# Batched transposed matmul on one core: loading the first batch of a ahead of the first pair of b, and opening the critical section through GpSimd

## Chip, cores, metric

One NeuronCore of one Trainium2 chip. The metric is the device time of one execution in microseconds (us), as the median of several runs; it is about 1.8 us longer than the span that the profiler records (124.78 us and 123.0 us for the same execution of the kernel before). Ratios are the mean time of one kernel's fast runs over that of the other's fast runs of the same rounds, so not quite the ratio of the medians that are quoted beside them.

## The reference

```python
batch, m, k, n = 16, 512, 512, 512
a: (batch, k, m) float32;  b: (batch, n, k) float32
return np.matmul(a.transpose(0, 2, 1), b.transpose(0, 2, 1)).astype(np.float32)
```

It reads 16.8 MB of a and 16.8 MB of b and writes 16.8 MB: 50.33 MB.

## The kernel before

Sixteen batches. b comes in pairs of batches (2.1 MB, rows of 16 KB), a in single batches (1.05 MB, rows of 8 KB). VectorE casts b to bf16, TensorE transposes it, VectorE copies the transpose back; ScalarE casts a; TensorE multiplies; ScalarE and VectorE copy the products out, and a pair of outputs is stored at once. There are buffers for 4 batches of a, 3 pairs of b and 5 pairs of outputs. Everything is in one critical section, a part of the program that one engine opens and closes for all of them, and in which the engines wait for each other by hand-written semaphores (counters). A transfer is asked for by an "issue" on SyncE's or ScalarE's queue, and has "landed" when its semaphore says so. The parts that matter here (cuts are marked):

```python
    with tc.tile_critical():                       # the section; opened and closed by SyncE by default
        ...
        def run_sp(sp):                            # SyncE issues all loads and the last stores
            for i in range(B):
                for p in ([0] if i == 0 else [(i + 1) // 2] if i % 2 and i + 1 < B else []):
                    if p >= PAIRS:
                        sp.wait_ge(turned, p - PAIRS + 1)
                    sp.dma_start(b_sb[p % PAIRS][:], b_v[p]).then_inc(b_in[p % PAIRS], 16)
                s, use = i % LOADS, i // LOADS
                if use:
                    sp.wait_ge(summed, MO * (i - LOADS) + 1)
                if i % 2 == 0 and i // 2 >= OUTS:
                    sp.wait_ge(o_out[i // 2 % OUTS], 16 * (i // 2 // OUTS))
                sp.dma_start(a_sb[s][:], a_v[i]).then_inc(a_in[s], 16)
            ...                                    # stores 5, 6, and 7 in two halves
            sp.reg_mov(all_stored, 16 * STORED)
        ...
        def run_act(act):
            cast_a(act, 0)
            for i in range(B - 1):
                cast_a(act, i + 1)
                copy_out(act, i, slice(2, 4), oa_go)
                j, odd = divmod(i - LAG, 2)        # LAG = 3
                if odd and 0 <= j < H - TAIL:
                    store(act, j)                  # stores 0 to 4, on ScalarE's queue
            ...
    nc.sync.wait_ge(stored, nc.sync.snap(all_stored))   # behind the section: the last stores
```

## Time and profile before

| | before |
|---|---|
| median, range of 6 runs | 124.97 us, 124.70 to 125.09 |
| PE / VectorE / ScalarE busy | 70% / 46% / 38% |
| moved, mean rate over the span | 50.33 MB, 409 GB/s |
| rate from 4 us to 120 us, in 2 us bins | 417 to 432 GB/s, one stretch at 403 |
| first issue, first packet, last packet, last landing, end | 0.949, 1.956, 121.450, 121.934, 122.985 us |

No compute engine is full and the DMA engines are, from the second of 40 equal slices of the span to the last but one. The table's last row is the useful one: the span is a start, 50.33 MB at the full rate, and an end.

### The profile page before, as it was taken

Reading aid. Unit: us, or ns where it says so; the run is one execution under the profiler, and the core shown is the slowest. Engines: PE = TensorE matmul, PEld = TensorE weight load, DVE = VectorE, ACT = ScalarE, POOL = GpSimd, SP = SyncE. Lnnn points to the kernel's source line nnn. Section 1 sums busy time; section 2 is a strip of 40 time slices with the busy share of each in tenths; the row PEclk is TensorE's granted clock in tenths of the full one; section 3 lists DMA queues with packets and bytes.
Section 4 is the critical chain, followed back from the end, with each engine's and each line's share of the span. In section 5 each row is a group of like instructions: output and inputs, shape, how many; then the busy total and the mean of one; then the engine's idle time right before and its main releaser. Section 6 shows DMA issues by size and latency. Waiting matters only on the chain. (4 is left out here: it accounts for less than half of the span.)

```text
span 123.0 us, 1086 instructions
## 1 busy us (share of the span) xinstructions
PE 86.1 (70%) x400; PEld 49.7 (40%) x400; DVE 56.4 (46%) x48; ACT 46.8 (38%) x34; POOL 0.7 (1%) x6
## 2 busy tenths in 40 slices
PE   0006497997999799779930799965992679979600
PEld 0006344642755464346410546442640526437300
DVE  0016368478295755917039107780719306171200
ACT  4003209537717903176300950329230490750300
POOL 2000000000000000000000000000000000000000
PEclk9999999999999999999995557999999558999995
DMA  4999999999999999999999999999999999999992
GB/s 91 394 400 458 400 424 456 429 394 456 426 397 448 434 376 432 426 440 440 416 421 429 458 408 418 429 426 437 453 397 432 426 426 426 429 426 426 429 424 115
DMA packets 5648, 50.33 MB, mean 409 GB/s; under 512 B 528, under 2 KB 528, under 8 KB 528
## 3 DMA queue, kind: packets, MB, share of 16 engines
q1 hardware_dynamic: 4288, 39.85, 77.2%
q10 hardware_dynamic: 1360, 10.49, 20.1%
HBM read 33.55 MB, written 16.78 MB: 409 GB/s over the span
## 5 line engine op out<-in xcount | busy, mean ns | idle before, releaser
L219 PE MATMUL o_ps<-bt_sb,a_bf 128*128 128x512 bf16 x256 | 65.1, 403 | 7.1 <-PEq L194 6.6
L135 ACT CAST a_bf<-a_sb 128x2048 bf16<-128x2048 f32 x16 | 30.4, 1900 | 40.8 <-DMA a_sb<-in_a_dram 40.8
L219 PEld LDWEIGHTS o_ps<-bt_sb,a_bf 128*128 128x128 bf16 x256 | 28.5, 115 | 37.5 <-issue 15.0
L205 PE MATMUL bt_ps<-identity,b_bf 128*128 128x128 f32 x144 | 24.3, 323 | 22.7 <-PEq L194 22.7
L144 DVE COPY o_sb<-o_ps 128x1024 f32<-128x1024 f32 x16 | 19.6, 1224 | 35.8 <-PE o_ps L219 35.8
L205 PEld LDWEIGHTS bt_ps<-identity,b_bf 128*128 128x128 f32 x144 | 22.2, 212 | 28.2 <-issue 27.2
L152 DVE CAST b_bf<-b_sb 128x2048 bf16<-128x2048 f32 x16 | 19.5, 1221 | 19.1 <-DMA b_sb<-in_b_dram 19.1
L144 ACT COPY o_sb<-o_ps 128x1024 f32<-128x1024 f32 (+1 forms) x17 | 16.4, 962 | 28.0 <-PE o_ps L219 28.0
L161 DVE COPY bt_sb<-bt_ps 128x1024 f32<-128x1024 f32 x16 | 19.5, 1216 | 3.1 <-PE bt_ps L205 3.1
L135 ACT ACT_TABLE_LOAD x1 | 1.3, 1283 | 0.9 <-SPq L51 0.9
L122 POOL TENSOR_SCALAR_AFFINE_SELECT identity<-identity 128x128 f32<-128x128 f32 x1 | 0.3, 294 | 0.2 <-POOL identity L120 0.2
L120 POOL MEMSET identity<- 128x128 f32 x1 | 0.2, 205 | 0.7 <-SPq L51 0.7
L265 POOL MEMSET const-bfloat16-1.0<- 128x1 bf16 x1 | 0.1, 102 | 0.0
L265 POOL MEMSET const-uint8-127<- 128x1 uint8 x1 | 0.1, 102 | 0.0
L265 POOL MEMSET const-float32-0.0<- 128x1 f32 x1 | 0.1, 99 | 0.2 <-issue 0.2
L265 POOL MEMSET const-float32-1.0<- 128x1 f32 x1 | 0.1, 99 | 0.0
## 6 DMA issues: line engine op xcount, KB each, us to landing
b_sb<-in_b_dram SPq DMA_DIRECT2D x8, 2048.0 KB, 20.4
a_sb<-in_a_dram SPq DMA_DIRECT2D x16, 1024.0 KB, 17.5
out_dram<-o_sb ACTq DMA_DIRECT2D x5, 2048.0 KB, 15.2
out_dram<-o_sb SPq DMA_DIRECT2D x2, 2048.0 KB, 13.6
out_dram<-o_sb SPq DMA_DIRECT2D x2, 1024.0 KB, 6.3
```

Source lines behind the costliest of these rows:

```text
L120: pool.memset(identity[:], 0.0).then_inc(id_go, 1)
L122: pool.affine_select(out=identity[:], in_=identity[:], compare_op=mybir.AluOpType.not_equal, fill=1.0, base=0, pattern=[[-1, P]], channel_ ...
L135: act.copy(a_bf[i % 2][:], a_sb[s][:]).then_inc(ac_go, 1)
L144: copy(o_sb[i // 2 % OUTS][:, i % 2, rm, :], o_ps[h][:, p, :]).then_inc(go, 1)
L152: dve.tensor_copy(b_bf[:, r, :], b_sb[p % PAIRS][:, r, :]).then_inc(bc_go, n)
L161: dve.tensor_copy(bt_sb[g][:].rearrange("p j (ni r) -> p j ni r", r=NR), bt_ps[:].rearrange("p j r (g ni) -> p g j ni r", g=2)[:, g],).the ...
L205: last = pe.transpose(bt_ps[:, j, r, :], w[:, r, j, :], identity[:])
L219: last = pe.matmul(o_ps[h][:, q, :], a_r[:, rk, 2 * h + q, :], bt_h[:, rk // 2, rk % 2, :], start=(rk == 0), stop=(rk == KO - 1),)
L265: nc = _bacc.Bacc("TRN2", target_bir_lowering=False, num_devices=1)
```

## The change

The intent as one can read it: let SyncE's first load go a little sooner by taking the section's opening off it, and let the small transfer go first.

```diff
-    with tc.tile_critical():
+    with tc.tile_critical(sync_engine=nc.gpsimd.engine):
@@ def run_sp(sp):
             for i in range(B):
+                if i == 0:
+                    sp.dma_start(a_sb[0][:], a_v[0]).then_inc(a_in[0], 16)
@@
-                sp.dma_start(a_sb[s][:], a_v[i]).then_inc(a_in[s], 16)
+                if i:
+                    sp.dma_start(a_sb[s][:], a_v[i]).then_inc(a_in[s], 16)
```

## The prediction

> **What bounds the kernel now.** I read the busy shares first, then the row of what the DMA engines moved, then the queue's own list of issues against that row, and last the two ends of the span.
>
> No compute engine is full, and the DMA row is:
>
> ```profile
> PE 86.1 (70%) x400; PEld 49.7 (40%) x400; DVE 56.4 (46%) x48; ACT 46.8 (38%) x34; POOL 0.7 (1%) x6
> ...
> DMA  4999999999999999999999999999999999999992
> GB/s 91 394 400 458 400 424 456 429 394 456 426 397 448 434 376 432 426 440 440 416 421 429 458 408 418 429 426 437 453 397 432 426 426 426 429 426 426 429 424 115
> ```
>
> The 16 DMA engines are at 90% or more in 38 of 40 slices; only the first and the last slice are not full. The GB/s row jitters because a transfer is counted in whole packets. Binned by 2 us from the packet records it is flat, 422 to 432 GB/s from 4 us to 120 us, whether the stretch holds loads alone or loads and stores, with one bin at 403 (44 to 46 us, where the ACT queue's first store joins). 50.33 MB over 427 GB/s is 117.9 us. The first packet starts at 1.96 us, the last ends at 121.45 us: 119.5 us, so that only 1.6 us of this stretch is not full-rate transfer (ramp at the front, unequal engines at the back). The chain of waits that ended last agrees by what it lacks: it covers 110.06 us to 116.5 us, 5% of the span, and the last 6 us belong to no engine, only to the last store.
>
> The ends, in windows of the trace (columns: busy time of the five rows, clock, DMA share, GB/s):
>
> ```profile
> 0.00:2.00 2.00, 0.00 (x0) 0.00 (x0) 0.00 (x0) 1.10 (x1) 0.70 (x6) 1.00 0.13 33
> 2.00:4.00 2.00, 0.00 (x0) 0.00 (x0) 0.00 (x0) 0.18 (x1) 0.00 (x0) 1.00 0.89 238
> 4.00:6.00 2.00, 0.00 (x0) 0.00 (x0) 0.00 (x0) 0.00 (x0) 0.00 (x0) 1.00 0.97 410
> ...
> 116.50:119.00 2.50, 0.00 (x0) 0.00 (x0) 0.00 (x0) 0.01 (x1) 0.00 (x0) 1.00 1.00 423
> 119.00:121.00 2.00, 0.00 (x0) 0.00 (x0) 0.00 (x0) 0.00 (x0) 0.00 (x0) 0.61 0.85 360
> ```
>
> So the time is: when the first transfer starts + 50.33 MB at the full rate + whatever time the DMA engines stand without work + the last store's completion (121.45 to about 121.93 us) + the closing barrier (to 123.0 us). The change can act on the first and the third term alone, as the bytes are the same.
>
> **What the Trainium skill says.** "DMA: Bandwidth & Descriptors", section "Where 436 GB/s comes from", gives 435 GB/s as the ceiling of the fabric and about 358 GB/s as a core's HBM limit; the trace's 427 GB/s sits 2% under the first and well over the second, so here the first is the one to measure by, and there is nothing left to gain in the rate. The same page, "Issuing engines are not separate DMA queues", says that transfers of all issuers run on the same 16 engines and interleave. The trace agrees: at 46 to 48 us the two queues moved 219 and 208 GB/s, 427 together. Hence what counts is the total backlog, not which queue has it. "Perfetto Trace Analysis", section "Per-engine timelines", says that a sequencer-only instruction shows only its execution, and that its semaphore's way to the other engines is hidden behind it; I read that way from the starts: the section's entry no-op of SyncE starts at 0.720 us and the branches that wait for it on ScalarE and GpSimd start at 0.755 and 0.758 us, 35 to 38 ns later.
>
> **The change, part 1: who opens the section.** In the records of before: GpSimd closes the opening barrier at 0.612 us, SyncE comes out of it at 0.655 us, runs the entry no-op at 0.720 us, then its own branch on that semaphore at 0.795 us, and issues the first load at 0.949 us (154 ns after the branch). With GpSimd as the opener, its no-op can run about as long after 0.612 us as SyncE's ran after 0.655 us (65 ns), at about 0.68 us; 35 ns on, SyncE may pass its branch, at about 0.72 us, in place of the no-op it no longer has. The first load then goes out at 0.72 + 0.154 = 0.87 us, some 75 ns earlier, and as DMA is the bound all of it should come off the end: **-0.08 us**. At the other end the section is left at 117.0 to 117.3 us, while SyncE waits for the last store until 121.95 us; a slower exit through GpSimd (its drains take 34 to 99 ns against SyncE's 7) lies within that 4.6 us: **0**.
>
> **Part 2: a's batch 0 ahead of b's pair 0.** All loads go down SyncE's queue in order, the first seven (10.49 MB) without a wait:
>
> ```profile
> 0.95 0.39 SPq L97 DMA_DIRECT2D b_sb<-in_b_dram  x1
> 1.39 0.42 SPq L104 DMA_DIRECT2D a_sb<-in_a_dram  x1
> 1.86 0.42 SPq L97 DMA_DIRECT2D b_sb<-in_b_dram  x1
> ...
> 8.81 2.36 DVE L152 CAST b_bf<-b_sb 128x2048 bf16<-128x2048 f32 x2 [8.81 <-DMA b_sb<-in_b_dram]
> ...
> 11.25 1.90 ACT L135 CAST a_bf<-a_sb 128x2048 bf16<-128x2048 f32 x1 [9.06 <-DMA a_sb<-in_a_dram]
> 13.83 1.23 DVE L161 COPY bt_sb<-bt_ps 128x1024 f32<-128x1024 f32 x1 [2.66 <-PE bt_ps L205]
> ```
>
> Before, b's pair 0 lands at 8.79 us and a's batch 0 at 11.23 us. The long path to the first matmul is b's: cast 2.36 us, 16 transposes, copy to 15.06 us, first matmul at 15.55 us; a's cast is done by 13.15 us and waits. Swapped, a's batch lands near 11.23 - 2.10 MB / 427 GB/s = 6.3 us and b's pair near 11.2 us (both minus the 0.08). The path through b is 1.05 MB / 427 GB/s = **2.4 us later**, first matmul at about 17.9 us. From b's pair 1 on (landing 16.14 us) the order is as before. By itself this part delays the computation; the question is whether DMA ever feels it.
>
> What feels it first is each issue that waits for PE. I set the bytes issued before each issue against the bytes moved by then. The lowest backlogs: 4.7 MB at 16.7 us (a's batch 4, which waits for batch 0's first product), 4.4 MB at 27.2 us, 4.1 MB at 37.7 us. Issuing each 2.4 us later costs 2.4 x 0.427 = 1.03 MB of backlog, which leaves 3.1 MB at the thinnest, 7 us of work. A DMA issued into a busy stream needs well under that to begin (1.0 us from issue to first packet at the start). So no gap: **0** in this stretch.
>
> From about 50 us the delay dies out, because computation is then the faster one (PE rests 30% of the span; DVE waits 5.3 us for b at 63.6 us, ACT 8.2 us for a at 67.8 us and 6.6 us at 96.9 us). Issues there are tied to landings, not to computation: store j leaves ACT when a's batch 2j+5 has landed (51.69, 67.85, 82.30, 96.93 us, each at a cast's start), and a's batches 10, 12, 14 leave when stores 0, 1, 2 have landed.
>
> **The tail** has the smallest margin: backlog 1.22 MB at 108.35 us, 1.65 MB at 112.24 us and 0.87 MB at 116.54 us, the last store's issue. 0.87 MB is 2.0 us of transfer, minus about 1.0 us from issue to first packet: DMA would run dry if the last product came more than 1.0 us later. That product hangs on a's batch 13 (lands 96.9 us). In queue order, 31.46 MB of loads and at most four stores (8.39 MB) can lie ahead of it, 39.85 MB; before, 40.04 MB had been moved by 96.93 us, so it is already at its latest. A first store that is issued up to 2.4 us later can only put loads ahead of stores, never behind. So the tail should end no later: **0**.
>
> Sum: 124.96 - 0.08 = 124.88 us; I say 124.85, as smaller 8 KB rows first may shorten the ramp by a few hundredths (packets of 16 KB took 0.9 to 1.9 us at first and 0.61 us later), which I can't work out.
>
> **Rivals.**
> (a) The late start runs through to the end, +2.4 us, 127.3 us (1.9% slower). For it: computation in the first 50 us is paced by PE at about 10.5 us a pair with hardly a rest, so the delay is not absorbed early, and 1.0 us is little room at the end. Against it: the long waits for DMA from 60 us on. A partial form, of which up to 1 us comes through, gives 125.5 to 126.
> (b) Starting with a smaller transfer fills the queue worse: a's 1 MB is gone in 2.5 us, so if b's pair were issued late there would be a hole. Against it: b's issue follows 0.44 us after a's in the list above. It would cost 0.3 us at most, 125.2 us.
> (c) The shift rearranges loads and stores so that the tail gets better: first store later, loads sooner, products earlier. But the tail already has DMA at 423 to 431 GB/s to 119 us, so there is nothing to collect but the ragged last 0.8 us, 124.4 us at best.
> (d) The throttle: the granted clock falls to half in some slices (the eight matmuls at 99.12 us took 3.48 us, against 1.99 us elsewhere). If it falls at another point in the tail, PE could eat the 1.0 us of room: +0.5 to +1.5 us, by chance.
>
> **Range and chances.** The spread of three runs is 0.24 us; the main line says -0.1, (c) down to -0.5, (b) and the mild forms of (a) and (d) up to +0.6. So 124.3 to 125.5 us. 2% is 2.5 us: faster would need more than the whole 1.6 us that DMA is not at full rate, so 0.01; slower needs (a) in full and more, 0.03.
>
> **What would show it.** Right: the first issue at about 0.87 us; a's first cast waiting until about 6.3 us, b's until about 11.1 us, the first matmul at about 17.8 us; the 38 full slices stay; the last packets end at 121.2 to 121.5 us; backlog never under 3 MB before 60 us. Wrong: a hole in the DMA row after 4 us, or the last store issued more than 1 us later than 116.54 us with the end following it, or a first issue that isn't earlier.

## The result

124.91 us (124.53 to 125.05, 6 runs) against 124.97 us (124.70 to 125.09, 6 runs): ratio 0.9996, interval 0.998 to 1.0013, the same. Executions over 1.5% slower than the fastest of the same kernel are left out of the means.

The DMA rows of the page of the changed kernel, to be set beside those of before in the prediction (40 equal slices; tenths of DMA busy, then GB/s):

```profile
DMA  2999999999999999999999999999999999999993
GB/s 72 450 431 426 421 426 437 415 426 437 426 415 431 431 338 405 426 447 413 423 429 426 447 429 413 429 429 447 423 423 426 426 429 426 429 426 423 426 429 128
```

Still 38 full slices and no hole. But one slice, the 15th, shows 338 GB/s while its engines count as 90% busy: something slowed the packets there. The start of the changed kernel, in order of time (start, length, engine, line):

```profile
0.89 0.39 SPq L94 DMA_DIRECT2D a_sb<-in_a_dram  x1
...
5.71 1.90 ACT L139 CAST a_bf<-a_sb 128x2048 bf16<-128x2048 f32 x1 [3.54 <-DMA a_sb<-in_a_dram]
10.60 2.36 DVE L156 CAST b_bf<-b_sb 128x2048 bf16<-128x2048 f32 x2 [10.60 <-DMA b_sb<-in_b_dram]
...
17.39 2.90 PE L223 MATMUL o_ps<-bt_sb,a_bf 128*128 128x512 bf16 x12 [1.75 <-PEq L198]
```

And its two ends, beside the same windows of before in the prediction (the last column counts a packet whole in the window in which it starts, so single windows are rough):

```profile
0.00:2.00 2.00, 0.00 (x0) 0.00 (x0) 0.00 (x0) 1.11 (x1) 0.70 (x6) 1.00 0.22 33
2.00:4.00 2.00, 0.00 (x0) 0.00 (x0) 0.00 (x0) 0.18 (x1) 0.00 (x0) 1.00 0.70 270
4.00:6.00 2.00, 0.00 (x0) 0.00 (x0) 0.00 (x0) 0.29 (x1) 0.00 (x0) 1.00 1.14 483
...
119.00:121.00 2.00, 0.00 (x0) 0.00 (x0) 0.00 (x0) 0.00 (x0) 0.00 (x0) 1.00 0.94 397
```

The swap did what it had to: a's cast waits until 5.71 us in place of 11.25, b's until 10.60 in place of 8.81, and the first product starts at 17.39 us in place of 15.55, 1.84 us later. None of that reached the end.

To see what did, I split the span of each profile into terms that add up to it, worked out from the packet records of the trace (each packet's bytes spread evenly over its time) against a reference rate of 428 GB/s, at which 50.33 MB take 117.60 us. Ramp: what is lost from the first issue to 20 us. Stretch: what is lost from 40 to 60 us. Tail: what the last packet is late by, from 118 us on. Exit: from the last landing to the end of the span. Left out of the table: from 20 to 40 us all of these lose 0.12 us, from 60 to 118 us nothing (within 0.02), and from the last packet to its landing all take 0.47 to 0.49 us.

| profile | first issue | ramp | stretch | tail | exit | span |
|---|---|---|---|---|---|---|
| before | 0.949 | 2.079 | 0.133 | 0.577 | 1.051 | 122.99 |
| before, second look | 0.950 | 2.063 | 0.206 | 0.573 | 1.051 | 123.03 |
| entry alone | 0.885 | 2.113 | 0.068 | 0.547 | 1.198 | 123.01 |
| changed | 0.888 | 1.775 | 0.695 | 0.342 | 1.197 | 123.09 |
| changed, second look | 0.886 | 1.893 | 0.317 | 0.376 | 1.198 | 122.85 |
| order alone | 0.948 | 1.842 | 0.344 | 0.279 | 1.051 | 122.64 |
| changed, GpSimd waits last | 0.886 | 1.906 | 0.341 | 0.448 | 1.040 | 122.80 |

First issue and exit repeat to 3 ns and go with the entry; ramp, stretch and tail scatter by 0.03 to 0.4 us and, by these few profiles, go with the order. From the means of three profiles with b first and four with a first: first issue -0.06, ramp -0.23 (2.085 to 1.854), stretch +0.29 (0.136 to 0.424), tail -0.20 (0.566 to 0.361), exit +0.15 (first issue and exit by the entry alone, 0.949 to 0.888 and 1.051 to 1.197); together -0.06 us. The change is near zero as a sum of five terms that cancel, and only one of the five was forecast at its size.

Ramp and tail may be one thing. The records name no DMA engine, but a transfer counts up its semaphore 16 times, which I read as one count for each engine; the time between the first and the last of them then shows how far apart the 16 engines are. In the kernel before it is 1.10 us at the first load and still 1.05 us at 40 us; in the changed kernel it is 0.46 us at both. At the last store it is 0.98 and 0.77 us. So with a first the engines start less unevenly, and the last of them may have less to catch up. That this lasts to the end is not shown: in between the stores move the figure up and down, and the second look at the changed kernel had 0.80 us at 40 us and 0.99 us at the end.

### The profile page after: what moved, and what is told of

Read it like the earlier page. It is cut to its first block, busy times and chain, and to the rows that moved or that the text cites. A ratio compares the mean times of both kernels' runs of the same rounds, so it can differ in the third digit from the quotient of the medians.

```text
span 123.1 us, 1088 instructions
## 1 busy us (share of the span) xinstructions
PE 86.2 (70%) x400; PEld 49.3 (40%) x400; DVE 56.2 (46%) x48; ACT 46.9 (38%) x34; POOL 0.7 (1%) x6
## 2 busy tenths in 40 slices
DMA packets 5648, 50.33 MB, mean 409 GB/s; under 512 B 528, under 2 KB 528, under 8 KB 528
## 5 line engine op out<-in xcount | busy, mean ns | idle before, releaser
L223 PE MATMUL o_ps<-bt_sb,a_bf 128*128 128x512 bf16 x256 | 66.4, 410 | 9.4 <-PEq L198 9.0
L209 PE MATMUL bt_ps<-identity,b_bf 128*128 128x128 f32 x144 | 23.3, 313 | 21.0 <-PEq L198 21.0
L209 PEld LDWEIGHTS bt_ps<-identity,b_bf 128*128 128x128 f32 x144 | 21.5, 211 | 26.7 <-issue 25.9
```

Of the source, the lines that this page charges most:

```text
L209: last = pe.transpose(bt_ps[:, j, r, :], w[:, r, j, :], identity[:])
L223: last = pe.matmul(o_ps[h][:, q, :], a_r[:, rk, 2 * h + q, :], bt_h[:, rk // 2, rk % 2, :], start=(rk == 0), stop=(rk == KO - 1),)
```

## The experiments

Twelve runs, all correct, all but two looks with timed rounds. "Ratio" is against the kernel before, of the same rounds.

### The two parts apart: entry alone, order alone

```diff
 # entry alone: the kernel before with
-    with tc.tile_critical():
+    with tc.tile_critical(sync_engine=nc.gpsimd.engine):
```

> The section opened through GpSimd, the loads in the old order. Theory (the time of the change is a sum of small terms that cancel): the first load is issued at 0.89 us in place of 0.949, its first packet 0.06 us earlier; but SyncE, after the last store has landed, runs two more waits on the section's exit (366 ns from its wait's end to its last drain, against 219 ns before), so the two cost 0.09 us net: ratio 1.000 to 1.001, about 125.05 us. The moved bytes at 20 us stay at about 7.29 MB (7.26 of before plus 0.06 us of transfer), so no better ramp. Rival (the entry alone carries the gain and the exit is hidden): 0.06 us faster, with 219 ns at the end.

Measured 124.97 us against 124.86, ratio 1.0009 (0.999 to 1.0029). First issue 0.885 us; from the landing of the last store to the end of the span 1.198 us in place of 1.051. The time alone could not settle 0.09 us; the two instants do, as they are the same to 3 ns in every profile with this entry and SyncE's last wait.

The records of the opening say why it is 0.06 and not the 0.075 us forecast: GpSimd's no-op starts at 0.694 us, 81 ns after it closed the barrier at 0.613 (I took 65 ns, SyncE's figure); SyncE's branch follows 40 ns later at 0.734 us, and the load 154 ns later at 0.888 us, as before. The exit is seen in the groups of instructions behind the section. First those of SyncE's queue in the kernel before, then in the changed kernel (count, least/median/most ns, first and last start):

```profile
L276 SPq DRAIN  x3: 7/7/7, 122.1 to 122.4; - x3
L276 SPq COMPARE_BRANCH  x2: 32/32/33, 0.8 to 122.0; - x2
L276 SPq EVENT_SEMAPHORE  x2: 17/17/17, 122.3 to 122.9; - x2
```

```profile
L280 SPq EVENT_SEMAPHORE  x4: 17/22/28, 122.1 to 123.0; - x4
L280 SPq DRAIN  x3: 7/7/7, 122.2 to 122.5; - x3
L280 SPq COMPARE_BRANCH  x2: 33/33/33, 0.7 to 121.9; - x2
```

The last branch is the wait for the last store. Before, SyncE, as the section's closer, had gathered the other engines' exit semaphores at 117.2 us, beside the transfer. Now GpSimd gathers them, and SyncE must still learn of them: two more semaphore waits, from 122.1 us on, stand behind the last landing, on the path (they are two of the four EVENT_SEMAPHORE of the second list; before, SyncE has two in all). From the branch to SyncE's last drain ahead of the closing barrier it takes 366 ns in place of 219 (121.907 to 122.273 us; before, 121.951 to 122.170).

> The new order of the loads, opened through SyncE as before. Theory: the ramp is better with 8 KB rows ahead of the 16 KB rows; at 20 us about 7.40 MB have been moved, against 7.26 MB (0.3 us ahead), the first issue is back at 0.95 us, the end costs 219 ns again. If the slow stretch at 44 to 48 us of the changed kernel (0.24 MB lost against before between 40 and 60 us) belongs to the later first store, it shows here too and the time is about 124.8 us; rival (that stretch is chance): no loss there and about 124.6 us, ratio 0.997.

```diff
 # order alone: the changed kernel with
-    with tc.tile_critical(sync_engine=nc.gpsimd.engine):
+    with tc.tile_critical():
```

Measured 124.74 us against 124.86, ratio 0.9989 (0.9971 to 1.0007). 7.366 MB moved at 20 us, near the 7.40 expected; first issue 0.948 and exit 1.051 are back. It has a slow stretch too, of 0.34 us, between the two theories' figures; the sum of its terms against the mean of b first (-0.24 + 0.21 - 0.29) is -0.3 us for this one profile, and -0.15 us with the means over the four profiles with a first.

### The exit taken off the path

```diff
-    all_stored = nc.sync.alloc_register("all_stored")
+    all_stored = nc.gpsimd.alloc_register("all_stored")
@@ run_sp: sp.reg_mov(all_stored, ...) goes; run_pool: pool.reg_mov(all_stored, 16 * STORED) comes
-    nc.sync.wait_ge(stored, nc.sync.snap(all_stored))
+    nc.gpsimd.wait_ge(stored, nc.gpsimd.snap(all_stored))
```

> The changed kernel with the wait for the last store moved from SyncE to GpSimd, which also closes the section. Theory (the new exit puts two waits on SyncE behind the last landing): SyncE's drains and exit waits now run at about 118 us, beside the last store, and from the landing of the last store to the end of the span about 0.15 to 0.2 us less pass than in the changed kernel (1.0 us after the landing at most, against 1.14); time 124.7 us, ratio 0.998. Rival (the exit costs nothing): the same time from landing to end as in the changed kernel.

Measured 124.64 us (124.58 to 124.69) against 124.86, ratio 0.9977 (0.996 to 0.9995): the lowest ratio of all, with an interval that leaves out 1, though by a quarter of a per cent. The same kernel with one small store more, further below, did not show that gain again (1.0001), so the gain in time is not safe; the exit is. The landing-to-end time is 1.040 us, 0.157 us less than in the changed kernel, as the theory expected of the difference. SyncE's drain out of the section has moved beside the transfer, here in its group of instructions:

```profile
L51 SPq DRAIN  x1: 123/123/123, 115.2 to 115.2; - x1
```

So the engine that opens the section and the one that waits last should be the same: SyncE for both takes 1.051 us from the landing to the end, GpSimd for both 1.040, one of each 1.197 to 1.198. Which one it is matters less.

### What makes the ramp: row size or tensor

```diff
 # the kernel before, with the first pair of b in two transfers of 8 KB rows
-                    sp.dma_start(b_sb[p % PAIRS][:], b_v[p]).then_inc(b_in[p % PAIRS], 16)
+                    if p == 0:
+                        for x, s0 in ((0, b_half), (1, b_in[0])):
+                            r = slice(x * NR // 2, (x + 1) * NR // 2)
+                            sp.dma_start(b_sb[0][:, r, :], b_v[0][:, r, :]).then_inc(s0, 16)
+                    else: ...                      # as before
@@ cast_b: the first half waits for b_half, the second for b_in[0]
```

> The kernel before with the first pair of b loaded in two transfers of 8 KB rows, each with its own semaphore; the order of the tensors as before, opened through SyncE. Theory (the ramp is a matter of the row size of the first transfer, not of which tensor it is): 7.40 MB moved at 20 us, as with a's batch ahead, and the first transposes start near 8 us in place of 10.2 us, with no later start of the computation. Time 124.6 to 124.9 us. Rival (the gain comes with the order): 7.26 MB at 20 us, as before.

Measured 124.97 us against 124.86, ratio 1.0012 (0.9992 to 1.0032). 7.341 MB moved at 20 us, ramp 1.898 us: most of what a's batch first gives (1.854), with b still first. So which tensor comes first matters little to the ramp; the form of the first transfers does. This edit halved the rows and the transfers together (8 KB and 1.05 MB in place of 16 KB and 2.1 MB), so which of the two counts was not told apart. In the records of before, the first packets of 16 KB took up to 1.92 us, where 0.61 us is usual; with 8 KB rows first they took up to 1.21 us in the changed kernel. The first transposes start at 7.53 us and the first product at 13.73 us, 1.8 us sooner than before, and the end does not move for that either. The time is not better, against what I expected: this profile lost 0.36 us in the stretch and 0.69 us in the tail.

### How much of a late start is hidden

```diff
 # n = 2 and n = 4 batches of a ahead of the first pair of b
-                    sp.dma_start(a_sb[0][:], a_v[0]).then_inc(a_in[0], 16)
+                    for f in range(n):
+                        sp.dma_start(a_sb[f][:], a_v[f]).then_inc(a_in[f], 16)
-                if i:
+                if i >= n:
```

> The changed kernel with two batches of a ahead of the first pair of b, so that the computation starts another 1.05 MB / 428 GB/s = 2.45 us later than in the changed kernel. Theory (the backlog of 3.2 MB hides a late start): first product matmul near 19.8 us in place of 17.4, lowest backlog before 60 us about 2.2 MB, DMA row without a hole, time within 0.5 us of the kernel before, ratio 0.998 to 1.003. Rival (a late start runs through to the end): 127.3 us, ratio 1.019.

Measured 124.87 us against 124.81, ratio 1.0001 (0.9985 to 1.0017). First product at 19.92 us, lowest backlog (bytes issued and not yet moved, by finished packets) before 60 us 2.16 MB: both as expected, and the start, now 4.4 us later than in the kernel before, is hidden, within the interval of about 0.2 us either way. The profiled run, 125.18 us, lost 1.05 us in the stretch, of which more below.

> All four of the first batches of a ahead of the first pair of b: b lands near 17.9 us, first product matmul near 24.7 us, 7.3 us later than in the changed kernel. Theory: 7.3 us cost 3.15 MB of backlog, so of the changed kernel's lowest backlog of 3.21 MB (at 39.6 us) 0.1 MB is left, at about 47 us: too little to cover the 1 us from issue to first packet, so DMA runs dry near 36 and 47 us, by 1 to 2.5 us in all; time 125.5 to 127.5 us. Rival (a late start runs through): 132 us. Rival (DMA never feels it): 124.9 us.

Measured 128.88 us against 124.81, ratio 1.0327 (1.028 to 1.0374). First product at 24.76 us. The direction of the theory is right, its size too small. Windows of the profile (busy times of PE, PEld, DVE, ACT, POOL; clock, DMA share, GB/s):

```profile
27.00:29.00 2.00, 1.57 (x7) 0.56 (x5) 2.00 (x2) 0.40 (x1) 0.00 (x0) 1.00 0.90 274
...
36.00:41.00 5.00, 4.13 (x22) 2.40 (x21) 3.49 (x3) 3.94 (x4) 0.00 (x0) 1.00 0.92 341
...
47.00:54.00 7.00, 6.13 (x34) 3.79 (x33) 3.92 (x4) 4.43 (x3) 0.00 (x0) 1.00 0.98 328
```

The backlog fell to 0.79 MB at 25.9 us, 0.70 MB at 36.4 us and 0.91 MB at 46.9 us, and after each of the three the rate is down. 1.73 us are lost between 20 and 40 us and 1.98 us between 40 and 60 us, where 0.12 and 0.42 are usual with a first. I had expected the engines to run dry below a backlog worth 1 us (0.43 MB); the rate already suffers with 0.7 to 0.9 MB queued. Here is the limit of the buffering: the changed kernel's 1.84 us cost nothing that the runs show, 4.4 us neither, 9.2 us cost 4 us.

### How much room the end has

```diff
             copy_out(act, B - 1, 2, last_go)
+            for x in range(4):
+                act.copy(spare[:, x, :], o_ps[1][:, 0, :])
             copy_out(act, B - 1, 3, last_go)
```

(The copies go to a spare buffer that nobody reads.)

> The changed kernel with four copies of 128x512 into a spare buffer on ScalarE ahead of the last copy: 4 x 0.59 us = 2.3 us later issue of the last store, at 118.8 to 119.6 us. Theory (the end has about 1 us of room): DMA runs dry for about 1 us, the time grows by 0.8 to 1.6 us, to 125.7 to 126.5 us, ratio 1.007 to 1.013. Rival (no room, the end hangs on the last product): 2.3 us, 127.2 us. Rival (more room than that): no change.

Measured 125.02 us (124.70 to 125.60) against 124.81, ratio 1.0008 (0.9986 to 1.003): less than expected in the median, and close to the lower end of what was expected in the profiled run, whose time was 125.60. In it the last store is issued at 118.755 us, with 0.01 MB left to move, and the engines stand:

```profile
116.00:118.00 2.00, 0.57 (x3) 0.07 (x1) 0.00 (x0) 2.00 (x5) 0.00 (x0) 1.00 1.05 442
118.00:119.00 1.00, 0.00 (x0) 0.00 (x0) 0.00 (x0) 0.73 (x2) 0.00 (x0) 1.00 0.22 90
119.00:120.00 1.00, 0.00 (x0) 0.00 (x0) 0.00 (x0) 0.00 (x0) 0.00 (x0) 1.00 0.55 229
120.00:122.00 2.00, 0.00 (x0) 0.00 (x0) 0.00 (x0) 0.00 (x0) 0.00 (x0) 0.93 0.99 410
```

From issue to the store's first packet took 0.84 us with the engines empty. So the room, estimated as the backlog at the last issue over 428 GB/s less 0.84 us, is 0.87 MB, 1.2 us, in the first profile of before and 0.64 MB, 0.66 us, in that of the changed kernel. It differs from run to run, because the last issue does: 115.02 and 116.54 us in the two looks at before, 117.28 and 114.74 us in the two at the changed kernel, whose spans lie 0.23 us apart. That would explain why the four copies seem hidden in some of the timed runs and not in others. I read the scatter as the throttle's: at 100 to 108 us the granted clock (the share of its full clock that TensorE was given) was 0.72 in the look that issued last (117.28 us), 0.85 in the next (116.54) and 1.00 in the two others. No run tested it.

### The slow stretch at the first store

In every profile, if only slightly in some with b first, loads get slower some 2 to 3 us after ScalarE has issued the first large store, and recover within 2 us of that store's first packet (with four batches of a ahead it cannot be told from the holes). The window in which it lies, in the kernel before and then in the changed one:

```profile
44.00:48.00 4.00, 3.92 (x22) 2.35 (x21) 3.49 (x3) 0.88 (x1) 0.00 (x0) 1.00 1.00 410
```

```profile
44.00:48.00 4.00, 4.00 (x24) 2.67 (x24) 1.80 (x2) 1.11 (x1) 0.00 (x0) 1.00 0.95 330
```

And with two batches ahead:

```profile
46.00:50.00 4.00, 3.93 (x26) 2.94 (x26) 1.78 (x3) 1.64 (x1) 0.00 (x0) 1.00 0.99 311
```

The engines are busy, at 0.99 of their time, and move 311 GB/s: the packets of the loads take longer, half of them over 0.41 us and up to 0.74 us for 8 KB in place of 0.31, so this is no hole for want of work. The store's own packets take 0.31 us from the first on. Three experiments asked for the cause.

```diff
 # with GpSimd waiting last, and ScalarE's queue used once at the start
         def run_act(act):
+            act.dma_start(warm[:], a_v[0][:, 0, 0:P]).then_inc(warm_in, 16)
```

> The changed kernel with GpSimd's wait for the last store, and ScalarE issuing one load of 64 KB, which nobody reads, at the start, so that ScalarE's queue has been used once before the first store. Question: what is the slow stretch before the first store's first packet (0.07 to 0.70 us lost between 40 and 60 us in six profiles, packets of loads at 0.46 us for 8 KB in place of 0.31). Theory (it is the first use of the second queue): less than 0.1 us lost there, and 0.2 us less in all than without the load, 124.5 us, ratio 0.996. Rival (it is the first writing to memory, or chance): 0.1 to 0.7 us lost as before, time 124.7 us.

Measured 125.12 us against 124.81, ratio 1.0027 (1.0012 to 1.0042). The stretch lost 0.46 us as before, so it is not the first use of the queue. The small load itself cost more than its bytes: the ramp went to 2.24 us.

```diff
 # with GpSimd waiting last, and a small early write to the output
         def run_act(act):
+            act.wait_ge(id_go, 2)
+            act.dma_start(out_v[0][:, 0, 0:P], identity[:]).then_inc(early, 16)
@@ ahead of store 0
+                    act.wait_ge(early, 16)
```

> The changed kernel with GpSimd's last wait, and a store of 64 KB from the identity tile into the output at the start through ScalarE (overwritten by the first real store, which waits for it). Theory (the slow stretch is the first writing to the output of all): under 0.1 us lost between 40 and 60 us. Rival (it comes with the first large store, whatever went before, as the early load on the same queue took nothing from it): 0.3 to 0.5 us lost, time 124.7 to 125.1 us.

Measured 124.88 us against 124.85, ratio 1.0001 (0.9978 to 1.0023). The stretch lost 0.62 us: not the first writing either, at least not of 64 KB.

```diff
 # with GpSimd waiting last
-    LAG = 3
+    LAG = 1
```

> The changed kernel with GpSimd's last wait and every store of ScalarE two batches sooner (a lag of 1 in place of 3): the first store at about 33 us, with more than 4 MB of loads behind it. Theory (the stretch grows as the backlog at the first store shrinks: 6.2 MB gave 0.07 to 0.36 us, 4.5 to 5.2 MB 0.34 to 0.70 us, 4.0 MB 1.05 us): backlog about 4.2 MB, loss of 0.5 us or more, now near 35 us. Rival (it goes with the time since the start): 0.1 us or less. Time 124.4 to 125.2 us.

The first store left at 33.4 us with 4.9 MB queued (4.2 expected), and the stretch moved with it: 0.61 us lost from 20 to 40 us, where 0.12 is usual, and none from 40 to 60 us. So it goes with the first large store, not with the time since the start. The time was far off what I wrote: 126.99 and 128.78 us in its two fast runs (two more, 129.09 and 129.37, count as slow by their time) against 124.85. The DMA engines stood still near the end:

```profile
108.00:111.00 3.00, 3.00 (x15) 1.84 (x14) 1.92 (x2) 0.00 (x0) 0.00 (x0) 0.76 0.95 401
111.00:112.00 1.00, 1.00 (x6) 0.55 (x5) 0.00 (x0) 0.81 (x1) 0.00 (x0) 1.00 0.04 16
112.00:113.00 1.00, 1.00 (x6) 0.48 (x5) 0.00 (x0) 1.00 (x2) 0.00 (x0) 1.00 0.00 0
113.00:114.00 1.00, 1.00 (x6) 0.50 (x5) 0.98 (x1) 1.00 (x1) 0.00 (x0) 1.00 0.00 0
```

The reason is the rule that the prediction used for the tail, turned round. ScalarE's cast of a's batch 13, in the changed kernel and then with the lag of 1:

```profile
96.93 1.90 ACT L139 CAST a_bf<-a_sb 128x2048 bf16<-128x2048 f32 x1 [5.15 <-DMA a_sb<-in_a_dram]
```

```profile
101.66 1.90 ACT L139 CAST a_bf<-a_sb 128x2048 bf16<-128x2048 f32 x1 [5.21 <-DMA a_sb<-in_a_dram]
```

With the lag of 3, at most four stores can be moved ahead of that batch; with the lag of 1, a fifth left at 86.98 us, before the batch had landed, and took its share of the engines. The batch lands 4.7 us later, the computation behind it is as long as ever, and there are no stores left to fill the time: the last store, issued between 114.7 and 117.3 us in the looks at the other two kernels, is issued at 122.1 us.

Whether the new order makes the stretch longer stays open. Three profiles with b first lost 0.07 to 0.21 us, four with a first 0.32 to 0.70 us (and 0.46 us with the late tail); but b first in two halves lost 0.36 us. A smaller backlog at the first store goes with a larger loss only loosely: 6.2 MB gave 0.07, 0.13 and 0.36 us, 5.6 MB 0.21, 5.2 MB 0.70, 0.62 (the early write) and 0.46, 4.5 MB 0.32 to 0.46, 4.0 MB 1.05. A rival that no run tested is which loads are under way then. In the two profiles that lost least, all packets of loads between the store's issue and its first packet were b's of 16 KB (89 and 95 of them); where a's of 8 KB were among them, 0.21 to 1.05 us were lost. But b first in two halves had 16 KB packets alone there too (86), and lost 0.36 us, so this does not settle it.

### Second looks

> The kernel before once more, unaltered, for a second look at its profile. Theory (the slow stretch between 40 and 60 us grows with the later first store): again about 0.1 us lost there, ramp to 20 us of 2.08 to 2.11 us after the first issue. Rival (the stretch is chance): anything from 0.1 to 0.7 us.

124.81 us in one run; ramp 2.063 (just under the range), stretch 0.206 (twice the theory's, and within the rival's range), first issue 0.950, exit 1.051 us.

> The changed kernel once more, unaltered. Theory: 0.3 to 0.7 us lost between 40 and 60 us, ramp 1.75 to 1.9 us, first issue at 0.888 us and 1.197 us from the last landing to the end, both to the nanosecond or two. Rival (chance): under 0.2 us lost.

124.64 us in one run; ramp 1.893, stretch 0.317, first issue 0.886, exit 1.198 us: all as the theory had it, the stretch barely. The clocks, 0.922 and 0.934, are no lower than in the other profiles.

## Why the prediction was right, point by point

- **DMA is the bound, and only start, holes and end can move.** Held: the rate from 4 us to 118 us is the same in both kernels outside the stretch (421 to 432 GB/s in 2 us bins, but for 417 at 4 to 6 us before, where the prediction has 422 as the least). The total, 124.85 forecast and 124.91 measured, lies 0.06 us apart.
- **Entry, -0.075 us.** Right in kind; 0.061 us, since GpSimd's no-op came 81 ns after its barrier and not 65.
- **Exit, 0.** This step failed. I took the exit to be over at 117.3 us as before, 4.6 us ahead of the last store's landing. In fact, with GpSimd as the closer, SyncE's part of the exit comes after SyncE's own wait for the last store: +0.147 us, more than the entry gave. Entry alone and the moved last wait show it from both sides.
- **A later computation, 0.** Right: 1.84 us later (2.4 forecast; b's pair landed at 10.57 us and not 11.2, as the ramp was better and the 16 engines lay less far apart), lowest backlog 3.21 MB (3.1 forecast), no hole. The sign that the backlog would never be under 3 MB held in this look only: the three other profiles of the table with a first fell to 2.6 MB at 41.3 to 41.4 us, as their first 16 product matmuls took 5.4 to 6.5 us in place of 3.80, with a granted clock shown as 1.00, which stays unexplained. The two experiments with more of a ahead show that this holds up to 4.4 us and not at 9.2 us. So rival (a) fell.
- **The ramp, a few hundredths.** The right sign, the size wrong by much: -0.23 us. That the form of the first transfers is the reason was shown by b in halves; whether it is the rows, as I wrote, was not. Rival (b), a worse start with the smaller transfer, fell with it.
- **The stretch, 0.** Not seen at all, although the 403 GB/s bin of before, which the prediction quotes, is by its place the same thing: +0.29 us by the means, from a cause that the runs do not settle.
- **The tail, 0.** It ended no later, as argued, though the last issue came 0.74 us later in the profiled run, which rival (d) had allowed for. But it ended 0.2 us less late against the full rate. Rival (c) had a ragged end to collect in mind, but from a better order of loads and stores; that the engines start less unevenly with a first may be the reason, and is not shown.

So the time was forecast well and the terms only in part: the missed ones, +0.15, +0.29, -0.20 and about -0.2, cancelled, which is luck. The parts built apart agree with the terms, though this is a check of consistency only, as their own profiles went into the means: +0.09 us worked out from them for the entry alone, +0.11 measured (0.0009 of 124.9); -0.15 for the order alone, -0.14 measured; -0.22 for the order with GpSimd waiting last, -0.29 measured; each within its interval.

## What to carry to other kernels

In a kernel whose DMA engines are never idle, add up start, ramp, holes, tail and exit before judging a change; a reordering that delays the computation by microseconds cost nothing here as long as the backlog stayed at 2.16 MB or more, and did cost where it fell to 0.7 to 0.9 MB. If the engine that opens a section is changed, look at what the engine that waits last has to do after that wait; make both the same engine. And which load the last products hang on, and how many stores may go ahead of it, is worth more here (2 to 4 us by the lag) than all that the change touched.

## What the Trainium skill lacked or had wrong

- "DMA: Bandwidth & Descriptors", section "Specifications", gives about 0.6 us to the first byte for a transfer issued from SyncE or ScalarE. Here it took 1.01 us from issue to first packet at the start (0.949 to 1.956 and 0.888 to 1.899 us), and 0.84 us late in a run with the engines empty. Counted from the end of the issue's own record, which is 0.34 to 0.39 us long, it is 0.62 and 0.50 us, near the page's figure; the page does not say from where it counts.
- The same page, "Where 436 GB/s comes from", says that for HBM to SBUF transfers the HBM side, about 358 GB/s, binds, though the same note calls a measurement of 425 GB/s near the fabric's rate; "HBM Reference", section "Specifications (TRN2)", says that a core streaming alone measures about 425. The runs agree with the second: one core moved 427 GB/s for 115 us, with loads alone and with loads and stores (whether the other core of its pair was idle is not on record).
- I found no page with the slowness of the first packets: packets of 16 KB took up to 1.92 us at the start against 0.61 us later, and first transfers of 1.05 MB with 8 KB rows made the ramp 0.2 us shorter.
- Nor one with the slow stretch ahead of the first large store's packets: many packets of loads at 0.4 to 0.7 us for 8 KB in place of 0.31 us, while the store's own packets take 0.31 us; 0.07 to 1.05 us lost in all.
- Nor one that says where a critical section's exit waits land: with GpSimd as the closer and SyncE as the last waiter they cost 0.147 us behind the last store.
